# Token-major RWKV values for two groups at once, with the one-token shift through DRAM scratch, in a one-core hybrid attention layer

## The chip, the core and the metric

One core of one Trainium2 chip runs the whole layer as one program. The metric is the device time of one execution in microseconds (us), and of several runs the median. The engines are TensorE (PE in the profile, its weight loads PEld), VectorE (DVE), ScalarE (ACT), GpSimd (POOL) and SyncE (SP), which here only issues DMAs. Each engine works through its own instructions in the order in which the program holds them, and waits on semaphores for the others.

## The reference

A layer of 256 tokens by 2048 features: RMS norm, one wide projection `w_in`, three branches (block attention, an RWKV-7 time mix, attention to a memory), a gated merge and an output projection. The change touches the RWKV branch alone:

```python
def token_shift_lerp(p, mu):
    prev = jnp.pad(p, ((0, 0), (1, 0), (0, 0)))[:, :-1]
    return p + (prev - p) * mu

# rwkv7_time_mix, cut
r = token_shift_lerp(r, mu_r); k = token_shift_lerp(k, mu_k); v = token_shift_lerp(v, mu_v)
...
def step(state, inp):
    r_t, w_t, k_t, v_t, a_t, b_t = inp
    sa = jnp.einsum('bhvk,bhk->bhv', state, a_t)
    state = state * w_t[:, :, None, :] + sa[..., None] * b_t[:, :, None, :] + v_t[..., None] * k_t[:, :, None, :]
    return state, jnp.einsum('bhvk,bhk->bhv', state, r_t)
...
bonus = jnp.sum(rh * kh * r_k, axis=-1, keepdims=True) * vh
```

So v is a projection of the normed input, each token mixed with the token before it by a weight per feature, and is then needed with tokens on the partitions in the recurrence's products and in the bonus.

## The kernel before

**Weights and products.** Every projection is a list of jobs, each cut into chunks of 512 KB of weights. A chunk is loaded by SP (L259, tile `raw`, three buffers), split on ACT into a high part (L270) and on VectorE into the low rest (L273, tile `wt`, four buffers), and multiplied on PE into `pm` tiles of PSUM. In a feature-major job (mode "fm") the weight is stationary and the tokens stream: for each 128 rows one matmul of 512 columns (L308) and one of 256 (L309), over four row blocks and two column halves a chunk. In a wide job the tokens are stationary and 512 weight columns stream three times (L306): 12 matmuls a chunk, and the result has tokens on the partitions.

**Steps and lanes.** After each chunk (`issue_mm`) the loop calls `step_lanes`, which lets every lane, a Python generator, emit its next piece of work; `yield 3` lets three chunks pass. So the order on each engine is the order of emission, and a lane that waits for a flag only emits later.

**The RWKV groups.** Six groups of 256 features (four heads). Per group there are feature-major jobs for R, K and V, whose evacuation (`rkv_evac`, `shift_lerp`) adds the two PSUM parts on POOL (L323), subtracts neighbouring tokens along the free dimension on POOL (L435) and finishes the lerp on VectorE (L431). `pairs_lane` builds decays and keys and ends in a burst of transposes on PE: the squares and r*k sums (L590), then in two tiles V (L599) and both halves of BK (L600, L601), copied to `tok` by ACT (L602) and VectorE (L604). `rw_lane` then makes the gram products (L622, evacuated by VectorE, L626 and L627), sends a 32-column block of them through DRAM (`d1`, `NB`, L652, L663), solves it by forward substitution in many small VectorE instructions (L674, L678, eight steps), and goes on to the products that read V (`from_v` L641, state L751, output L763) and to the group norm (transposes L780, subtraction `Y` L790, L803 on POOL, bonus L805). All small products and transposes share four PSUM tiles named `psd`; a tile is free when its reader is through. `attn_a` holds one from its last product (L876, L878) until its gate is there (L881).

Of the kernel before, what the change touches and what calls it, by code (L numbers as in the profile page):

```python
# [11 lines left out]
FT = mybir.dt.float32  # L12
# [9 lines left out]
NG = 6  # L22
# [16 lines left out]
def tile_hybrid(ctx: ExitStack, tc: tile.TileContext, x, mem, rel_bias, norm_g, mem_norm_g, w_in,  # L39
# [87 lines left out]
    prow2 = load_params((("mur", mu_r, 12), ("muk", mu_k, 12), ("muv", mu_v, 12), ("a0", a0, 12),  # L127
# [248 lines left out]
    def open_p1():  # L376
# [6 lines left out]
        for k in ("XF", "X64", "S"):  # L383
            pool.memset(E[k], 0.0)
        for k in ("lw", "la"):
            E[k] = rw.tile([96, 256], FT, name=k + "_t")

    msk = const.tile([128, 2, 128], FT, name="msk")
    ones = const.tile([128, 1], FT, name="ones")
    fd = dram.tile([HA, 385], FT, name="fd")  # L390
# [61 lines left out]
    def rkv_evac(g, nm, mu):  # L452
# [10 lines left out]
        return f  # L463

# [41 lines left out]
    def pairs_lane(g):  # L506
# [53 lines left out]
        tok = rw.tile([128, 2, 4, 128], FT, name="tok", bufs=2)  # L560
# [22 lines left out]
        yield from wait(("V", g))  # L583
        yield 1
# [9 lines left out]
        v = St.pop(("V", g))  # L594
        for q in range(2):
            p = ps_side()
            pv = p.rearrange("p (a c) -> p a c", a=4)
            for c in range(2):
                pe.transpose(pv[:, c], v[:, q, c * 128:(c + 1) * 128], ident)  # L599
            pe.transpose(pv[:, 2], BK[:, q, 0, 128:256], ident)  # L600
            pe.transpose(pv[:, 3], BK[:, q, 0, 0:128], ident)  # L601
            act.activation(tok[:, q, 0:3], pv[:, 0:3], AF.Copy)  # L602
            for h in range(2):
                dve.tensor_scalar(tok[:, q, 3, 64 * h:64 * h + 64], pv[:, 3, 64 * h:64 * h + 64],  # L604
                                  nb[:, 0, q, h:h + 1], None, op0=OP.mult)
# [4 lines left out]
    def rw_lane(g, AR, BK, tok, nb, bs, esc):  # L610
        rw, GS, XF, X64 = (E[k] for k in ("rw", "GS", "XF", "X64"))
        S = E["S"]
        halves = [slice(64 * h, 64 * h + 64) for h in range(2)]
# [17 lines left out]
        def from_v(c):  # L631
# [4 lines left out]
            for q in range(2):  # L636
# [3 lines left out]
                for h, rows in enumerate(halves):  # L640
                    pe.matmul(pv[:, 2 * q + h], GS[:, c * 4 + 2 * q + h, 2], tok[:, q, c, rows], start=(c == 0), stop=True,  # L641
# [62 lines left out]
        for s in D4[0:2]:  # L704
            act.activation(X64[s, :, s], XN[s], AF.Copy)
        W = from_v(0)
# [29 lines left out]
        for c in range(2):  # L736
# [9 lines left out]
            if c == 0:  # L746
                p = ps_side()
                pv = p[:, 0:128].rearrange("p (q v) -> p q v", q=2)
                for q in range(2):
                    for h, rows in enumerate(halves):  # L750
                        pe.matmul(pv[rows, q], tok[:, q, 2, rows], tok[:, q, 0, rows], start=True, stop=False)  # L751
                        pe.matmul(pv[rows, q], tok[:, q, 3, rows], W[:, 1, q * 2 + h], start=False, stop=True)
# [5 lines left out]
            for q in range(2):  # L758
                if c:
                    pe.matmul(pv[:, q], S[:, q], AR[:, q, 1, 1], start=True, stop=False, skip_group_check=True)  # L760
                for h, rows in enumerate(halves):
                    u = c * 4 + 2 * q + h
                    pe.matmul(pv[rows, q], tok[:, q, c, rows], GS[:, u, 3], start=(c == 0), stop=False,  # L763
# [534 lines left out]
```

## Time and profile before

| | |
|---|---|
| median of three runs | 1477.9 us (1477.35 to 1479.44) |
| profiled execution | 1478.3 us, of which the span from first to last instruction is 1476.5 us |
| PE, PEld, DVE, ACT, POOL busy | 98%, 83%, 64%, 51%, 12% of the span |
| granted TensorE clock | 0.997 of the 2.4 GHz level, over the whole span |
| moved by DMA | 258.9 MB |

Everything the change touches lies in the first half, up to about 740 us; what follows (memory attention, merge, output) is the same text in both kernels. The page's first two parts say who is busy, the chain says what ended last, the table of waits says for whom an engine stood still, and the timeline gives starts, from which the pace of back-to-back instructions is read: a matmul's own duration overlaps its neighbours', the distance of two starts does not.

### The profile page before, as it was taken

What the parts mean: (1) busy time and instruction counts of PE and PEld (TensorE: products, weight loads), DVE (VectorE), ACT (ScalarE), POOL (GpSimd) and SP (SyncE); (2) the same over time, 40 slices, a digit from 0 to 9 for tenths busy, and PEclk for the clock granted to TensorE, in tenths of its full rate; (3) what the DMA queues carried; (4) which work ended last, traced back from release to release, by engine and by line L of the source; (5) the groups of instructions that cost most, each with busy time, mean ns of one, the idle gap of its engine ahead of it and who ended that gap; (6) DMA issues with size and microseconds to landing.
All of it is one profiled execution on the core that took longest, in us unless ns stands there. A gap on an engine that the chain in (4) does not pass through costs nothing.

```text
span 1476.5 us, 22151 instructions
## 1 busy us (share of the span) xinstructions
PE 1449.2 (98%) x8315; PEld 1222.3 (83%) x8315; DVE 946.2 (64%) x1855; ACT 747.3 (51%) x1122; POOL 181.8 (12%) x252
## 2 busy tenths in 40 slices
PE   7999999999999999999999999999999999999997
PEld 6887888888888788788888888888888888888887
DVE  5778697796795786784666555655545545545555
ACT  5546546466456456445666454643443444444443
POOL 4312202212212222211100000000000000000011
PEclk9999999999999999999999999999999999999999
DMA  5665555456465465465575555566556556555753
GB/s 180 192 179 163 159 147 169 143 167 173 133 184 151 134 172 159 135 178 158 162 221 187 172 169 174 167 196 192 187 188 195 188 187 194 188 188 192 262 200 130
DMA packets 207968, 258.88 MB, mean 175 GB/s; under 512 B 28172, under 2 KB 146596, under 8 KB 207220
## 3 DMA queue, kind: packets, MB, share of 16 engines
q1 hardware_dynamic: 201872, 247.11, 54.5%
q10 hardware_dynamic: 4164, 6.71, 1.3%
q0 software_dynamic: 1824, 3.65, 0.8%
q8 instruction: 65, 1.06, 0.3%
q14 instruction: 43, 0.35, 0.1%
HBM read 253.74 MB, written 6.05 MB: 176 GB/s over the span
## 4 chain that ended last, share of the span: by engine, by line
PE 89%; DVE 4%; DMA 2%; ACT 1%; issue 1%; POOL 1%; SPq 0%; ACTq 0%; DVEq 0%
PE pm L306 43%; PE pm L308 24%; PE pm L309 12%; PE psd L622 2%; DVE wt L273 1%; DMA raw<-in_w_in_dram 1%; DVE fs_t L674 1%; PE psd L641 1%; PE psd L1037 1%; PE psd L743 1%; DMA NB<-d 1%; PE psd L154 1%; DMA x_sb<-in_x_dram 1%; ACT wt L270 1%; DVE X L678 1%
## 5 line engine op out<-in xcount | busy, mean ns | idle before, releaser
L273 DVE TENSOR_TENSOR wt<-raw,wt 128x1024 fp32r<-128x1024 f32 (+1 forms) x451 | 559.1, 1242 | 437.4 <-ACT wt L270 433.8
L270 ACT ACTIVATE wt<-raw 128x1024 fp32r<-128x1024 f32 (+1 forms) x452 | 477.2, 1057 | 494.0 <-PE pm L306 256.5
L308 PE MATMUL pm<-hT,wt 128*128 128x512 f32 (+1 forms) x1632 | 587.1, 402 | 0.0
L309 PE MATMUL pm<-hT,wt 128*128 128x256 f32 (+1 forms) x1632 | 458.5, 281 | 3.5 <-DVE wt L273 3.4
L308 PEld LDWEIGHTS pm<-hT,wt 128*128 128x128 f32 (+1 forms) x1632 | 305.7, 187 | 76.3 <-issue 4.2
L306 PE MATMUL pm<-wt,hT 128*128 128x512 f32 x1440 | 335.4, 391 | 0.0
L306 PEld LDWEIGHTS pm<-wt,hT 128*128 128x128 f32 x1440 | 268.6, 188 | 57.6 <-issue 1.7
L309 PEld LDWEIGHTS pm<-hT,wt 128*128 128x128 f32 (+1 forms) x1632 | 307.5, 188 | 6.2 <-DVE wt L273 6.0
L306 PE MATMUL pm<-wt,mg 128*128 128x512 f32 (+1 forms) x384 | 79.3, 367 | 0.0
L306 PEld LDWEIGHTS pm<-wt,mg 128*128 128x128 f32 x384 | 65.7, 189 | 12.5
L1183 POOL MEMSET sso<- 128x16 f32 x1 | 0.1, 117 | 607.0 <-PE pm L306 607.0
L674 DVE TENSOR_TENSOR fs_t<-X,NB 128x30 f32<-128x30 f32 (+13 forms) x354 | 64.9, 223 | 7.5 <-DMA NB<-d 7.1
L306 PE MATMUL pm<-wt,yas 128*128 128x512 f32 x288 | 67.6, 395 | 0.0
L306 PE MATMUL pm<-wt,ybs 128*128 128x512 f32 x288 | 67.6, 395 | 0.0
L323 POOL TENSOR_TENSOR lraw<-lraw,et 128x256 f32<-128x256 f32 (+1 forms) x38 | 45.1, 1207 | 167.2 <-ACT lraw L322 167.2
L306 PEld LDWEIGHTS pm<-wt,ybs 128*128 128x128 f32 x288 | 54.3, 188 | 12.6
L306 PEld LDWEIGHTS pm<-wt,yas 128*128 128x128 f32 x288 | 54.3, 188 | 12.7
L317 ACT ACTIVATE et<-pm 128x256 f32<-128x256 f32 (+1 forms) x112 | 42.6, 382 | 40.3 <-PE pm L309 37.6
L678 DVE TENSOR_TENSOR X<-X,fs_t 128x30 f32<-128x30 f32 (+13 forms) x354 | 56.3, 194 | 0.6
L306 PE MATMUL pm<-wt,mT 128*128 128x512 f32 x192 | 45.8, 395 | 0.0
L308 PE MATMUL pm<-mT,wt 128*128 128x512 f32 x128 | 45.4, 395 | 0.0
L306 PE MATMUL pm<-wt,ycs 128*128 128x512 f32 x192 | 45.3, 395 | 0.0
(299 smaller groups left out, 1324.3 us busy)
## 6 DMA issues: line engine op xcount, KB each, us to landing
raw<-in_w_in_dram SPq DMA_DIRECT2D x320, 512.0 KB, 3.7
raw<-in_w_mem_kv_dram SPq DMA_DIRECT2D x32, 512.0 KB, 3.5
raw<-in_w_out_dram SPq DMA_DIRECT2D x32, 512.0 KB, 4.4
raw<-in_w_proj_a_dram SPq DMA_DIRECT2D x24, 512.0 KB, 4.2
raw<-in_w_proj_b_dram SPq DMA_DIRECT2D x24, 512.0 KB
raw<-in_w_proj_c_dram SPq DMA_DIRECT2D x16, 512.0 KB, 4.4
NB<-d SPq DMA_DIRECT2D x24, 128.0 KB, 3.4
fr<-fd ACTq DMA_DIRECT2D x6, 385.0 KB
```

The source lines that it names most:

```text
L154: pe.transpose(pv[:, a, t], src[:, t, (k + a) * 128:(k + a + 1) * 128], ident)
L270: act.activation(w[:, :, 0], r, AF.Copy)
L273: eng.tensor_tensor(w[:, :, 1], r, w[:, :, 0].bitcast(FT), OP.subtract)
L306: pe.matmul(ps[:, 0:j.n], l, r, start=first and n == 0, stop=last and n == 2)
L308: pe.matmul(ps[0:j.m], hi, both, start=first, stop=last, skip_group_check=True)
L309: pe.matmul(ps[0:j.m, 256:512], lo, top, start=False, stop=last, skip_group_check=True)
L317: act.activation(t, ps[0:j.m, 256:512], AF.Copy)
L323: pool.tensor_tensor(j.dst[f], j.dst[f], t, OP.add)
L622: pe.matmul(pv[h][:, w].rearrange("p x t -> p (x t)"), BK[rows, q, c, w * 128:(w + 1) * 128], AR[rows, q, c].rearrange("p x t -> p (x t)") ...
L641: pe.matmul(pv[:, 2 * q + h], GS[:, c * 4 + 2 * q + h, 2], tok[:, q, c, rows], start=(c == 0), stop=True, skip_group_check=True)
L674: dve.tensor_tensor(t, X[:, k0:8, c:c + 1].to_broadcast([128, m, hi - lo]), NB[:, lo:hi, c].rearrange("p (o n) -> p o n", o=1).to_broadcas ...
L678: dve.tensor_tensor(X[:, k0:8, lo:hi], X[:, k0:8, lo:hi], t, OP.add)
```

## The change

V is computed by three wide jobs (`BJ`), each for two groups, placed after the K job of groups 0, 2 and 4, in place of six feature-major jobs; the attention jobs between are dealt out anew. `v_evac` copies the token-major result to `vt` on ACT. A new lane `v_lane` does the shift: SP stores `vt` to DRAM scratch from row 1 on (row 0 is zero, set once by four POOL DMAs), three steps later SP loads rows 0 to 255 back, so that each token meets the one before it; `mu_v` is loaded onto all partitions by a POOL DMA; three steps later POOL subtracts and multiplies, and two steps after that VectorE adds. V's four transposes per group are gone, and `tok` has two parts and one buffer, for which `pairs_lane` now waits for `half_free` of the group before; it no longer waits for V, `rw_lane` does, just ahead of `from_v`.

```diff
@@ open_p1, scratch
+        for v in vds:
+            for o in (0, 128):
+                pool.dma_start(v[0:1, o:o + 128].rearrange("o (q n) -> o q n", q=2), E["S"][0:1, :, 64:128])
...
+    vds = [dram.tile([257, 256], FT, name="vd%d" % i) for i in range(2)]
@@ new functions
+    def v_evac(g):
+
+        def f(ps, t):
+            if t == 0:
+                if g:
+                    force(("rw", g - 2))
+                for i in range(2):
+                    St["v", g + i] = E["rw"].tile([128, 2, 256], FT, name="vt", bufs=3)
+            for i in range(2):
+                act.activation(St["v", g + i][:, t], two(ps)[:, i], AF.Copy)
+            if t == 1:
+                add_lane(v_lane(g), 2)
+        return f
+
+    def v_lane(g0):
+        for g in (g0, g0 + 1):
+            vt = St["v", g]
+            sh = E["rw"].tile([128, 2, 256], FT, name="vsh")
+            mu = E["rw"].tile([128, 1, 256], FT, name="muv")
+            vd = vds[g % 2]
+            nc.sync.dma_start(vd[1:257].rearrange("(t p) v -> p t v", p=128), vt)
+            pool.dma_start(mu[:, 0], bass.AP(tensor=mu_v.tensor, offset=mu_v.offset + g * 256, ap=[[0, 128], [1, 256]]))
+            yield 3
+            nc.sync.dma_start(sh, vd[0:256].rearrange("(t p) v -> p t v", p=128))
+            yield 3
+            pool.tensor_tensor(sh, sh, vt, OP.subtract)
+            pool.tensor_tensor(sh, sh, mu.to_broadcast([128, 2, 256]), OP.mult)
+            yield 2
+            dve.tensor_tensor(vt, vt, sh, OP.add)
+            flags["V", g] = True
+            yield 1
@@ pairs_lane
-        tok = rw.tile([128, 2, 4, 128], FT, name="tok", bufs=2)
...
-        yield from wait(("V", g))
-        yield 1
+        if g:
+            yield from wait(("half_free", g - 1))
...
-        v = St.pop(("V", g))
+
+        tok = rw.tile([128, 2, 2, 128], FT, name="tok")
+        p = ps_side()
+        pv = p.rearrange("p (a q c) -> p a q c", a=2, q=2)
+        for a in range(2):
+            for q in range(2):
+                pe.transpose(pv[:, a, q], BK[:, q, 0, 128 * (1 - a):128 * (2 - a)], ident)
+        act.activation(tok[:, :, 0], pv[:, 0], AF.Copy)
         for q in range(2):
-            p = ps_side()
-            pv = p.rearrange("p (a c) -> p a c", a=4)
-            for c in range(2):
-                pe.transpose(pv[:, c], v[:, q, c * 128:(c + 1) * 128], ident)
-            pe.transpose(pv[:, 2], BK[:, q, 0, 128:256], ident)
-            pe.transpose(pv[:, 3], BK[:, q, 0, 0:128], ident)
-            act.activation(tok[:, q, 0:3], pv[:, 0:3], AF.Copy)
-            for h in range(2):
-                dve.tensor_scalar(tok[:, q, 3, 64 * h:64 * h + 64], pv[:, 3, 64 * h:64 * h + 64],
-                                  nb[:, 0, q, h:h + 1], None, op0=OP.mult)
+            dve.tensor_tensor(tok[:, q, 1].rearrange("p (h v) -> p h v", h=2), pv[:, 1, q].rearrange("p (h v) -> p h v", h=2),
+                              nb[:, 0, q].rearrange("p (h o) -> p h o", o=1).to_broadcast([128, 2, 64]), OP.mult)
@@ rw_lane, ahead of from_v(0); the products then read vt in place of tok
+        yield from wait(("V", g))
+        vt = St["v", g]
@@ the jobs
-               Job(w_in2, VB + c, 256, 16, hT, rkv_evac(g, "V", "muv"), add=pool),
...
-    for g, (a0_, a1_) in enumerate(((0, 3), (3, 5), (5, 8), (8, 10), (10, 13), (13, 16))):
-        jobs += RJ[4 * g:4 * g + 3] + AJ[a0_:a1_] + RJ[4 * g + 3:4 * g + 4 - (g == NG - 1)]
+    BJ = [Job(w_in2, VB + 512 * i, 512, 16, hT, v_evac(2 * i), mode="wide") for i in range(3)]
+    for g, (a0_, a1_) in enumerate(((0, 2), (2, 5), (5, 7), (7, 10), (10, 12), (12, 16))):
+        jobs += RJ[3 * g:3 * g + 2] + BJ[g // 2:g // 2 + 1 - g % 2] + AJ[a0_:a1_] + RJ[3 * g + 2:3 * g + 3 - (g == NG - 1)]
```

PE's order at group 4's burst of transposes, before (each line or pair of lines with `psd` is one tile; YT is the group norm of group 3):

```order
L309 MATMUL pm<-hT,wt 128x256
L780 MATMUL psd<-ident,YT 128x128 x4
L590 MATMUL psd<-ident,sg 128x128 x4
L590 MATMUL psd<-ident,R 128x128 x4
L599 MATMUL psd<-ident,V 128x128 x2
L600 MATMUL psd<-ident,BK 128x128
L601 MATMUL psd<-ident,BK 128x128
L599 MATMUL psd<-ident,V 128x128 x2
L600 MATMUL psd<-ident,BK 128x128
L601 MATMUL psd<-ident,BK 128x128
L308 MATMUL pm<-hT,wt 128x512
```

And after, where the burst stands between chunks of the wide V job of groups 4 and 5:

```order
L306 MATMUL pm<-wt,hT 128x512 x24
L818 MATMUL psd<-ident,YT 128x128 x4
L626 MATMUL psd<-ident,sg 128x128 x4
L626 MATMUL psd<-ident,R 128x128 x4
L636 MATMUL psd<-ident,BK 128x128 x4
L306 MATMUL pm<-wt,hT 128x512 x12
L658 MATMUL psd<-AR,BK 128x256 x8
```

The burst has four tiles instead of five and 16 transposes instead of 20; the gram products (L622 before, L658 after) follow one chunk later in both. In group 5 the scores of an attention group now stand right behind the burst.

SP's order in group 0, from the gram's block on, before:

```order
L652 DMA d_951<-GS 32x8x32 x4
L259 DMA raw<-in_w_in_dram 128x4x256
L663 DMA NB<-d_951 32x1024 x4
L259 DMA raw<-in_w_in_dram 128x4x256 x9
L682 DMA d_952<-X 256x1x32 x4
```

And after:

```order
L688 DMA d_853<-GS 32x8x32 x4
L259 DMA raw<-in_w_in_dram 128x4x256
L699 DMA NB<-d_853 32x1024 x4
L490 DMA vd_110<-vt 128x2x256
L259 DMA raw<-in_w_in_dram 128x4x256 x3
L493 DMA vsh<-vd_110 128x2x256
L259 DMA raw<-in_w_in_dram 128x4x256 x6
L718 DMA d_854<-X 256x1x32 x4
L490 DMA vd_111<-vt 128x2x256
```

The store of V stands behind the substitution's loads and three weight loads ahead of the shifted load.

VectorE's order in group 0 after the change, where the lerp's addition stands in the forward substitution (L710 and L714 are before's L674 and L678):

```order
L710 TENSOR_TENSOR fs_t<-X,NB 128x14 x2
L714 TENSOR_TENSOR X<-X,fs_t 128x7x2 x2
L498 TENSOR_TENSOR vt<-vt,vsh 128x512
L883 SCALAR_TENSOR_TENSOR as<-psd,bias 128x2x256
L884 SCALAR_TENSOR_TENSOR as<-psd,bias 128x2x128
L889 TENSOR_REDUCE amx<-as 128x2 x2
L273 TENSOR_TENSOR wt<-raw,wt 128x4x256
```

The addition and the softmax's first part stand ahead of a weight split between two column groups of the solve; so it is in group 0, and in groups 2 and 4 the addition lies in the solve too.

## Rows read from the trace of the kernel before

**Rows 1.** The page: busy time and share, and engines of the last chain.

```profile
PE 1449.2 (98%) x8315; PEld 1222.3 (83%) x8315; DVE 946.2 (64%) x1855; ACT 747.3 (51%) x1122; POOL 181.8 (12%) x252
PE 89%; DVE 4%; DMA 2%; ACT 1%; issue 1%; POOL 1%; SPq 0%; ACTq 0%; DVEq 0%
```

**Rows 2.** Whom PE waited for: us in total, times, longest.

```profile
PE pm L309 <- DVE wt L273: 3.4, 5, 0.9
PE psd L599 <- DVE Y L790: 3.4, 5, 0.9
PE psd L622 <- DVE GS L627: 2.3, 4, 0.6
```

**Rows 3.** Windows: stretch, length, busy PE, PEld, DVE, ACT, POOL, clock, DMA, GB/s.

```profile
110.00:131.00 21.00, 18.74 (x102) 15.09 (x101) 19.47 (x91) 13.52 (x24) 4.19 (x7) 1.00 0.52 157
```

**Rows 4.** Timeline of PE in a feature-major job, eight pairs apart.

```profile
427.53 0.39 PE L308 MATMUL pm<-hT,wt 128*128 128x512 f32 x1
...
430.36 0.40 PE L308 MATMUL pm<-hT,wt 128*128 128x512 f32 x1
```

**Rows 5.** Timeline of PE in a wide job: start, us, what, count.

```profile
402.72 16.62 PE L306 MATMUL pm<-wt,hT 128*128 128x512 f32 x72
419.18 0.60 PE L817 MATMUL psd<-ident,Y 128*128 128x128 f32 x4
```

**Rows 6.** Timeline of PE, group 3's burst; in brackets idle time and releaser.

```profile
390.13 0.38 PE L599 MATMUL psd<-ident,V 128*128 128x128 f32 x2
...
390.46 0.27 PE L601 MATMUL psd<-ident,BK 128*128 128x128 f32 x1
391.23 0.41 PE L599 MATMUL psd<-ident,V 128*128 128x128 f32 x2 [0.50 <-DVE Y L790]
```

**Rows 7.** Timeline of PE, group 4's burst and gram products.

```profile
493.83 0.38 PE L590 MATMUL psd<-ident,R 128*128 128x128 f32 x2
495.15 0.41 PE L599 MATMUL psd<-ident,V 128*128 128x128 f32 x2 [0.93 <-DVE Y L790]
...
501.15 1.10 PE L622 MATMUL psd<-AR,BK 64*128 64x256 f32 x6 [0.57 <-DVE GS L627]
```

**Rows 8.** Groups by line and shape: count, busy us, mean ns.

```profile
L431 DVE SCALAR_TENSOR_TENSOR V<-et,par,lraw 128x256 f32<-128x256 f32 x12 | 5.3, 482 | 6.3 <-POOL et L435 6.3
L604 DVE TENSOR_SCALAR tok<-psd,nb 128x64 f32<-128x64 f32 x24 | 5.2, 276 | 0.6
L473 DVE TENSOR_TENSOR zsa<-zsa,et 128x512 f32<-128x512 f32 x6 | 4.1, 683 | 0.0
L803 POOL TENSOR_TENSOR Y<-Y,lnw 128x512 f32<-128x512 f32 x6 | 8.2, 1362 | 87.3 <-issue 53.8 <-DVE Y L801 33.5
```

**Rows 9.** Timelines of VectorE and POOL around 112 us, group 0's solve.

```profile
111.59 0.31 DVE L678 TENSOR_TENSOR X<-X,fs_t 128x33 f32<-128x33 f32 x2
...
112.08 0.85 DVE L678 TENSOR_TENSOR X<-X,fs_t 128x33 f32<-128x33 f32 x2
112.85 0.88 DVE L674 TENSOR_TENSOR fs_t<-X,NB 128x30 f32<-128x30 f32 x2
...
112.14 1.52 POOL L323 TENSOR_TENSOR zsa<-zsa,et 128x256 f32<-128x256 f32 x2 [13.94 <-ACT zsa L322]
```

**Rows 10.** Whom PE waited for between 100 and 140 us.

```profile
PE pm L309 <- DVE wt L273: 2.2, 3, 0.9
```

**Rows 11.** DMA issues: count, size, median us from issue to landing.

```profile
out_dram<-xo SPq DMA_DIRECT2D x4, 256.0 KB, 2.7
...
wd<-in_rw_w_decay_dram POOLq DMA_DIRECT2D x6, 96.0 KB, 3.7
```

**Rows 12.** Timelines of POOL and PE at the start and in V's evacuation.

```profile
35.41 0.53 POOL L515 DMA_DIRECT2D wd<-in_rw_w_decay_dram  x1
42.17 1.03 PE L521 MATMUL psd<-lw_t,wd 96*128 96x256 f32 x4
68.62 6.26 POOL L323 TENSOR_TENSOR lraw<-lraw,et 128x256 f32<-128x256 f32 x2 [4.24 <-ACT lraw L322]
```

More of the change, by code (lines that the diff above doesn't have):

```diff
@@ L126, in tile_hybrid @@
     prow1 = load_params((("g", norm_g, 16),), "1", pool)
-    prow2 = load_params((("mur", mu_r, 12), ("muk", mu_k, 12), ("muv", mu_v, 12), ("a0", a0, 12),
+    prow2 = load_params((("mur", mu_r, 12), ("muk", mu_k, 12), ("a0", a0, 12),
                          ("kk", k_k, 12), ("ka", k_a, 12), ("rk", r_k, 12), ("lnb", lnx_b, 12), ("w0", w0, 12), ("mg", mem_norm_g, 16),
@@ L612, in rw_lane @@
         S = E["S"]
+        vt = None
         halves = [slice(64 * h, 64 * h + 64) for h in range(2)]
@@ L640, in from_v @@
                 for h, rows in enumerate(halves):
-                    pe.matmul(pv[:, 2 * q + h], GS[:, c * 4 + 2 * q + h, 2], tok[:, q, c, rows], start=(c == 0), stop=True,
+                    pe.matmul(pv[:, 2 * q + h], GS[:, c * 4 + 2 * q + h, 2], vt[:, c, 128 * q + 64 * h:128 * q + 64 * h + 64], start=(c == 0), stop=True,
                               skip_group_check=True)
@@ L750, in rw_lane @@
                     for h, rows in enumerate(halves):
-                        pe.matmul(pv[rows, q], tok[:, q, 2, rows], tok[:, q, 0, rows], start=True, stop=False)
-                        pe.matmul(pv[rows, q], tok[:, q, 3, rows], W[:, 1, q * 2 + h], start=False, stop=True)
+                        pe.matmul(pv[rows, q], tok[:, q, 0, rows], vt[:, 0, 128 * q + 64 * h:128 * q + 64 * h + 64], start=True, stop=False)
+                        pe.matmul(pv[rows, q], tok[:, q, 1, rows], W[:, 1, q * 2 + h], start=False, stop=True)
                 for rows in halves:
@@ L762, in rw_lane @@
                     u = c * 4 + 2 * q + h
-                    pe.matmul(pv[rows, q], tok[:, q, c, rows], GS[:, u, 3], start=(c == 0), stop=False,
+                    pe.matmul(pv[rows, q], vt[:, c, 128 * q + 64 * h:128 * q + 64 * h + 64], GS[:, u, 3], start=(c == 0), stop=False,
                               skip_group_check=True)
@@ L806, in rw_lane @@
                 Yq[:, c * 4:c * 4 + 4].rearrange("p (q h) v -> p q h v", q=2),
-                tok[:, :, c].rearrange("p q (h v) -> p q h v", h=2),
+                vt[:, c].rearrange("p (q h v) -> p q h v", q=2, h=2),
                 bs[:, c].rearrange("p q (h o) -> p q h o", o=1).to_broadcast([128, 2, 2, 64]), OP.mult)
```

## The prediction

> **What bounds the kernel now.** Read the page's busy shares and the chain that ended last first: TensorE is busy for 98% of the span, and 89% of the chain is TensorE, most of it the big products L306, L308 and L309 [rows 1]. So time comes off only where PE has fewer columns to stream or waits less. Next, who PE waits for: behind the start it waits 3.4 us for the weight split on VectorE (L273), 3.4 us at the V transposes (L599) for the group norm's subtraction (Y, L790) and 2.3 us at the gram products (L622) for their own evacuation [rows 2]. That is all a faster helper can win. The windows show the other side: in the stretches where VectorE runs the forward substitution (L674, L678), here 110 to 131 us, it is itself busy for 19.47 of 21.00 us [rows 3], and there the weight split is late. An engine with 64% over the span is a second bound in six places.
>
> **The V products (less by 2.0 us).** Six jobs of 32 pairs (512 columns, then 256) become three of 96 matmuls of 512; the columns are the same, the instructions fewer (384 to 288). The feature-major pace: from 427.53 to 430.36 us lie eight pairs, one chunk, 2.83 us [rows 4]. The wide pace: 72 matmuls from 402.72 to 419.18, 16.46 us, so 2.74 us for a chunk of twelve [rows 5]. 24 chunks either way: 24 x 0.083 = 2.0 us, on the path throughout.
> The rows give 229 ns for 512 columns and 354 ns for a 512 and a 256. The Trainium skill, "TensorE: Matmul & The Clock Gate", section "Back-to-back issue gap", has N / 2.4 + 2.5 ns for a matmul of N columns; by it a pair takes 325 ns and the same columns in 512s 324 ns, so an estimate of 0.3 us in all, and a sum of 5.1 instead of 6.8 us. The page does not have the 20 ns that the 256s cost here; the measured pace decides.
>
> **The V transposes (less by 2.6 us).** Three transposes pass from 390.13 to 390.46 us, 0.11 each [rows 6]. V's four per group go, 24 in all: 24 x 0.11 = 2.6 us. The matmuls that read v later (from_v, state, output) keep shape and number: nothing.
>
> **PSUM waits in that burst (less by 3.5 us).** Four side tiles exist. Before, the burst of transposes takes five: YT, two squared sums, two V/BK tiles. So the last one reuses YT's and stands until L790 has read it: 390.46 to 391.23 is 0.77 us where 0.11 would do [rows 6], 0.66 lost. In groups 4 and 5 an attention result holds one of the four (its lane waits for its gate), and already the fourth tile reuses YT's: two transposes from 493.83 should end at 494.05, and L599 starts at 495.15 [rows 7], 1.10 lost. Groups 1 to 3 lose 0.66, groups 4 and 5 lose 1.10: 4.2 us. The new burst takes four tiles. Groups 1 to 3: no reuse, nothing lost. Group 4: the order leaves the attention tile held across the burst, so the fourth still lands on YT's: 1.10 stays. Group 5: no tile is held any more, but the scores products now follow in the same step as a fifth tile; they come 0.44 us (four transposes) later, so 0.65 is lost there. 4.2 - 1.75 = 2.4 us less. The waits at L622 are the same shortage one chunk later, twice in group 4 and twice in group 5, 0.57 each [rows 2, 7]; group 4 keeps its two, group 5 loses its two: 1.1 less. Bounds of this term: nothing (each wait finds another place) and 6.5 (all of 4.2 and 2.3 gone).
>
> **VectorE and POOL (more by 1.3 us).** Per group VectorE loses two lerps (0.482 each) and four 64-column scalings (0.276) and gets two 128-column ones, priced between the 64-column row and L473's 0.68, taken as 0.35, nearer the first since the columns are few, and one 512-column addition at 0.68, as L473 [rows 8]: 2.07 off, 1.38 on. POOL loses two adds and a subtraction and gets two 512-column passes; the nearest row is L803 with 1.36 each [rows 8]. In sum no more than before, but they move: in groups 0, 2 and 4 the passes and the addition fall into the forward substitution. What that costs is in the trace: two POOL adds run from 112.14 to 113.66 and the pairs of small VectorE instructions beside them take 0.85 and 0.88 us instead of 0.31 [rows 9], about 0.55 for each add of 0.76, seven tenths of it. So two passes cost VectorE 0.7 x 2.72 = 1.9 us. Only group 0 is sure to have no cushion (2.2 of the 3.4 us by which PE waits for the split lie there [rows 10]); there 1.9 + 0.68 - 1.37 = 1.3 us reach PE. Lower bound -0.7 (the relief alone reaches PE, once), upper bound three groups at full lock, 3 x (2.72 + 0.68 - 1.37) = 6.1.
> The Trainium skill, "SBUF — State Buffer", section "Who interferes with whom", states that a VectorE instruction with two SBUF inputs and a GpSimd instruction that reads SBUF exclude each other for the whole instruction. By it the upper bound holds in each solve; the row shows seven tenths, so the trace bears the lock out with part of it hidden.
>
> **Round trip, SP and start (nothing).** SP gets a store of 256 KB, three weight loads later the shifted load. A 256 KB store landed in 2.7 us, a POOL load in 3.7 [rows 11]. Three weight loads are three chunks, 8.5 us: the load finds the store landed, and behind it only weight loads queue, which run six or seven chunks ahead of their use. In the order the first product that reads v (from_v) stands seven steps behind group 0's lerp, and further in the others. If the cover were gone: 2.7 us per trip. The store stands behind the substitution's loads in the queue, not ahead. At the start four small POOL DMAs go ahead of the lora sums, about 0.5 us each as the row of L515: w_decay2's load moves from 35.41 to 37.5, lands 3.7 us later [rows 11] at 41.2 and is read at 42.17 [rows 12]: hidden with 1 us left, otherwise at most 1 us.
>
> **Sum.** -2.0 - 2.6 - 3.5 + 1.3 = -6.8. The profiled execution took 1478.3 us, so 1471.5; it lay 0.4 above the median of the runs, so the forecast is 1471.1.
>
> **Rivals.**
> (1) The waits move instead of going: PE's PSUM waits stay at 6.5 us in new places (the scores in group 5 show the way). Then -2.0 - 2.6 + 1.3 = -3.3, 1474.6. For it: VectorE's work in the burst is hardly shorter; against it: four tiles for four uses in groups 1 to 3.
> (2) POOL and VectorE exclude each other in three solves: +6.1 in place of +1.3, that is -2.0, 1475.9. For it: VectorE is full there [rows 3]; against it: PE waits for the split in few places outside group 0.
> (3) Slower: the lerp's last addition (L498) stands in VectorE's strict order two steps, 2 x 2.83 = 5.7 us, behind POOL's first pass. If POOL's pair takes longer, VectorE stops mid-solve with the weight splits queued behind it, and PE starves. POOL did once need 6.26 us for two 256-column V adds beside a busy VectorE [rows 12]; at that rate two 512-column passes take 12.5 us, 6.9 too long, in groups 0, 2 and 4 20.6 us: -8.1 + 20.6 = +12.5, 1490.4. It decides from 9.4 us for the pair on (3.7 too long, three times: 3 us slower). Against it: L803's 1.36 and the idle POOL.
> (4) Only columns count for the V products, since they are the same: no gain from fewer instructions, -4.8, 1473.1. Against it: two paces read over eight pairs and 72 matmuls [rows 4, 5]. The formula in the Trainium skill's TensorE page, above, speaks for it.
> (5) The round trip is not hidden and the lane of a group waits for V, with the rest of its work bunched: about what was saved, 1478.
>
> **How the numbers follow.** No change means within 0.2%, about 3.0 us, so faster ends at 1474.9 and slower begins at 1480.9. Forecast 0.58; rival 1 0.13, half of it on either side of 1474.9; rival 2 0.16; rival 3 0.06; rival 4 0.05; rival 5 0.02. Faster 0.58 + 0.07 + 0.05 = 0.70, same 0.06 + 0.16 + 0.02 = 0.24, slower 0.06. The range: below, all PSUM waits gone and VectorE relieved would be -11.8; 1467.0 leaves that last corner out. Above, rivals 1 and 2 belong in, up to 1478.0.
>
> **What would show it.** V's L306 rows at 229 ns and 96 per job; no L599; the burst without idle time in groups 1 to 3, about 1.1 us at group 4's fourth tile, about 0.65 at group 5's scores; two L622-like waits instead of four; PE's wait for the split between 2.4 and 5 us, in group 0; POOL's two passes under 2 us each. Wrong would be: a wait of VectorE for POOL at L498, of SP for the store, or of PE for the split in groups 2 and 4 by more than 2 us each.

## The result: slower by 0.8%

| | before | after |
|---|---|---|
| median | 1477.7 us (1477.35 to 1479.44, four runs) | 1490.4 us (1487.8 to 1494.2, four runs) |
| ratio | | 1.0082 (95% interval 1.0067 to 1.0097) |
| profiled execution, span | 1478.3, 1476.5 us | 1494.2, 1492.5 us |

The forecast was 1471.1 us, range 1467.0 to 1478.0. The change costs 12.1 us (0.0082 x 1477.7) where 6.8 were to be gained. From the page of the kernel after, to be laid beside [rows 1]: PE's busy line and the shares of the chain that ended last.

```profile
PE 1451.5 (97%) x8195; PEld 1219.5 (82%) x8195; DVE 943.7 (63%) x1837; ACT 737.8 (49%) x1102; POOL 170.7 (11%) x249
PE 76%; DVE 11%; DMA 7%; ACT 2%; issue 2%; SPq 1%; POOL 0%; ACTq 0%; DVEq 0%
```

PE runs 120 matmuls fewer, VectorE is busy 2.5 us less, POOL 11 less: every engine has less to do. (PE's busy time is 2.3 us longer all the same, because stretches of it run at a lower clock, as shown below.) The chain tells the rest: PE's share falls from 89% to 76%, VectorE's rises from 4% to 11% and that of the DMAs from 2% to 7%. Work didn't grow, it became late. Whom PE waits for after the change (us in total, times, longest), against [rows 2]:

```profile
PE pm L309 <- DVE wt L273: 9.4, 11, 1.9
PE psd L736 <- DMA XN<-d: 3.1, 3, 2.5
PE pm L306 <- DVE wt L273: 2.8, 1, 2.8
PE psd L564 <- ACT XF L756: 1.9, 1, 1.9
PE psd L636 <- DVE BK L615: 1.9, 1, 1.9
PE psd L658 <- DVE GS L663: 1.1, 2, 0.6
PE psd L636 <- DVE Y L828: 0.9, 1, 0.9
...
PE psd L876 <- DVE Y L828: 0.5, 1, 0.5
```

The last three lines are the PSUM waits, where the prediction put them: group 4's fourth tile, two gram waits in place of four, group 5's scores. The first five are new or larger. The split (L273) is late for 12.2 us and not 3.4, in groups 0, 2, 3, 4 and 5; the solve's second hop through DRAM (XN), the copy of its result (XF) and the keys of group 0 (BK) are late where nothing was. A single number for the whole: over all pairs of neighbouring matmuls, take by how much the distance of their starts exceeds the median of their form, and add up those of more than 0.5 us. Behind PE's first 20 us that is 12.0 us before and 26.0 us after, called PE's lost time below.

Behind a stall comes a second loss. Four stretches of the windows in which PE is busy throughout (columns as in [rows 3], the clock is the third value from the end):

```profile
124.60:127.80 3.20, 3.20 (x11) 2.71 (x11) 1.26 (x2) 2.58 (x10) 0.00 (x0) 0.50 0.74 209
145.10:148.30 3.20, 3.20 (x12) 2.72 (x11) 3.20 (x6) 1.98 (x4) 2.57 (x3) 0.50 0.22 79
428.40:431.60 3.20, 3.20 (x9) 2.47 (x8) 3.20 (x15) 2.14 (x4) 0.00 (x0) 0.50 0.64 172
568.40:571.60 3.20, 3.20 (x12) 2.72 (x12) 1.87 (x2) 3.05 (x7) 2.89 (x5) 0.50 0.77 223
```

The granted clock is 0.50, 1.2 GHz, each time some us after PE stood for 2 to 3 us (the stall of 1.9 us for BK at 72 us left it at the full clock); pairs of products then start 0.64 us apart and not 0.35. The trace of before has no such stretch between its start and its end. The parts nearly add up: 14.0 us more of lost time, an estimate of 1.4 us for each of the four stretches shown (3.20 us at 0.35 / 0.64 of the pace), less the 4.6 us forecast for the V products and transposes, make 15.0 of the 16.0 us between the two spans. It is one trace: how many such stretches there are differs from run to run, and the median lies 3.7 us below this execution.

### The profile page after: what moved, and what is told of

Same layout as the page of the kernel before. It is cut to its first block, busy times and chain, and to the rows that moved or that the text cites. A ratio compares the mean times of both kernels' runs of the same rounds, so it can differ in the third digit from the quotient of the medians.

```text
span 1492.5 us, 21895 instructions
## 1 busy us (share of the span) xinstructions
PE 1451.5 (97%) x8195; PEld 1219.5 (82%) x8195; DVE 943.7 (63%) x1837; ACT 737.8 (49%) x1102; POOL 170.7 (11%) x249
## 4 chain that ended last, share of the span: by engine, by line
PE 76%; DVE 11%; DMA 7%; ACT 2%; issue 2%; SPq 1%; POOL 0%; ACTq 0%; DVEq 0%
PE pm L306 43%; PE pm L308 15%; PE pm L309 8%; DVE wt L273 4%; DVE fs_t L710 3%; DMA raw<-in_w_in_dram 3%; DVE X L714 2%; DMA NB<-d 1%; PE psd L658 1%; ACT wt L270 1%; DMA d<-GS 1%; PE psd L1075 1%; PE psd L781 1%; DMA XN<-d 1%; PE psd L154 1%
## 5 line engine op out<-in xcount | busy, mean ns | idle before, releaser
L273 DVE TENSOR_TENSOR wt<-raw,wt 128x1024 fp32r<-128x1024 f32 (+1 forms) x451 | 555.7, 1235 | 456.0 <-ACT wt L270 453.4
L308 PE MATMUL pm<-hT,wt 128*128 128x512 f32 (+1 forms) x1440 | 522.0, 404 | 0.0
L309 PE MATMUL pm<-hT,wt 128*128 128x256 f32 (+1 forms) x1440 | 407.9, 283 | 9.5 <-DVE wt L273 9.4
L306 PE MATMUL pm<-wt,hT 128*128 128x512 f32 x1728 | 407.3, 393 | 2.8 <-DVE wt L273 2.8
L306 PEld LDWEIGHTS pm<-wt,hT 128*128 128x128 f32 x1728 | 322.5, 189 | 73.8 <-issue 3.7
L308 PEld LDWEIGHTS pm<-hT,wt 128*128 128x128 f32 (+1 forms) x1440 | 272.4, 189 | 66.2 <-issue 2.4
L309 PEld LDWEIGHTS pm<-hT,wt 128*128 128x128 f32 (+1 forms) x1440 | 274.2, 190 | 14.1 <-DVE wt L273 13.8
L306 PE MATMUL pm<-wt,mg 128*128 128x512 f32 (+1 forms) x384 | 79.3, 367 | 0.0
L306 PEld LDWEIGHTS pm<-wt,mg 128*128 128x128 f32 x384 | 65.7, 189 | 12.5
L710 DVE TENSOR_TENSOR fs_t<-X,NB 128x30 f32<-128x30 f32 (+13 forms) x354 | 65.5, 224 | 11.6 <-DMA NB<-d 11.1
L306 PE MATMUL pm<-wt,yas 128*128 128x512 f32 x288 | 67.6, 395 | 0.0
L306 PE MATMUL pm<-wt,ybs 128*128 128x512 f32 x288 | 67.6, 395 | 0.0
L306 PEld LDWEIGHTS pm<-wt,ybs 128*128 128x128 f32 x288 | 54.3, 189 | 12.6
L306 PEld LDWEIGHTS pm<-wt,yas 128*128 128x128 f32 x288 | 54.3, 189 | 12.6
L714 DVE TENSOR_TENSOR X<-X,fs_t 128x30 f32<-128x30 f32 (+13 forms) x354 | 60.3, 206 | 0.6
L317 ACT ACTIVATE et<-pm 128x256 f32<-128x256 f32 (+1 forms) x100 | 38.0, 382 | 43.9 <-PE pm L309 39.2
L306 PE MATMUL pm<-wt,mT 128*128 128x512 f32 x192 | 45.8, 396 | 0.0
L306 PE MATMUL pm<-wt,ycs 128*128 128x512 f32 x192 | 45.3, 395 | 0.0
L306 PEld LDWEIGHTS pm<-wt,ycs 128*128 128x128 f32 x192 | 36.2, 189 | 8.4
```

The source lines that it names most:

```text
L273: eng.tensor_tensor(w[:, :, 1], r, w[:, :, 0].bitcast(FT), OP.subtract)
L306: pe.matmul(ps[:, 0:j.n], l, r, start=first and n == 0, stop=last and n == 2)
L308: pe.matmul(ps[0:j.m], hi, both, start=first, stop=last, skip_group_check=True)
L309: pe.matmul(ps[0:j.m, 256:512], lo, top, start=False, stop=last, skip_group_check=True)
L317: act.activation(t, ps[0:j.m, 256:512], AF.Copy)
L710: dve.tensor_tensor(t, X[:, k0:8, c:c + 1].to_broadcast([128, m, hi - lo]), NB[:, lo:hi, c].rearrange("p (o n) -> p o n", o=1).to_broadcas ...
```

## What the lane costs: four runs

The first theory was that the lane's transfers block SP and the solve's DRAM hops. The rivals: its sums on POOL and VectorE, or the new order of the attention jobs. One run drops the lane, one its transfers, one its sums, one moves the transfers.

```diff
 no_lane: v_lane only sets the flags
 no_trip:
-            nc.sync.dma_start(vd[1:257]...)  /  nc.sync.dma_start(sh, vd[0:256]...)
-            pool.tensor_tensor(sh, sh, vt, OP.subtract)
+            pool.tensor_tensor(sh, vt, vt, OP.subtract)
 no_lerp: the two pool.tensor_tensor and the dve.tensor_tensor of the lane are left out
 trips_early: both stores first, load 1 two steps later, sums two steps later, then load 2
```

> Leaves out the shift of the values: no store, no load, no mu row, no subtraction, product or addition of the lane; V goes to its users unshifted. Before is 1477.7 us, after 1490.4. Theory T (the lane's transfers stand between the two DRAM hops that end the solve, in groups 0, 2 and 4, and hold up these hops and the raw weights; after a stall PE runs at its lower clock): about 1477 us, since the stalls at 137 to 148, 563 and their low clock go, and those of group 0 at 120.7 and of group 3 at 424 stay. Rival O (the order of the attention work alone, scores and spread rows in the solves): 1486 or more, the lane is nearly free. Rival L (the lane's POOL and VectorE work in the solves): 1477 too, told apart by the next two runs.

> Leaves out the round trip: neither store nor load; the lane's subtraction, product, addition and mu row stay, on V itself (so the shift is left out). Theory T: about 1479 us, within 2 us of the run without the lane. Rival L: within 2 us of after, 1488 to 1491. Rival O: 1486 or more.

> Keeps both transfers and the mu row of the lane and leaves out its POOL subtraction and product and its VectorE addition (the shift is left out). Theory T: 1487 to 1490 us, since only 6 additions of 0.69 us go, half of them where VectorE is full. Rival L: about 1478. Rival O: 1486 or more, as in the other two runs.

> Computes all of it. Both stores at the lane's start, the first load two steps later, the second behind the first addition, so that no transfer of the lane stands between d<-X and XN<-d; VectorE's and POOL's work is the same and lies in the solve. Theory T: faster than after by the stalls behind the solves of groups 0, 2 and 4, 4 to 8 us, so 1482 to 1486; XN<-d lands in under 3 us again. Rivals L and O: 1490, or more, since more of the lane now falls in the solve.

| run | ratio to before | 95% interval |
|---|---|---|
| no_lane | 1.0041 | 1.0026 to 1.0056 |
| no_trip | 1.0076 | 1.0057 to 1.0094 |
| no_lerp | 1.0044 | 1.0031 to 1.0057 |
| trips_early | 1.0115 | 1.0102 to 1.0129 |

Each interval is 0.0013 to 0.0019 wide on either side, so the difference of two runs is known to about 0.002, 3 us. The theory fell. Without transfers the time hardly moves (0.0006); without the sums it moves as far as without the lane, 0.0038, 5.6 us. In trips_early both pairs of POOL passes lie in the solve, and it is slower by 0.0033. What the sums do is seen in the timelines of VectorE and POOL in the kernel after, group 0's solve, just where [rows 9] were read:

```profile
103.30 0.31 DVE L714 TENSOR_TENSOR X<-X,fs_t 128x33 f32<-128x33 f32 x2
103.53 1.43 DVE L710 TENSOR_TENSOR fs_t<-X,NB 128x30 f32<-128x30 f32 x2
104.88 1.39 DVE L714 TENSOR_TENSOR X<-X,fs_t 128x30 f32<-128x30 f32 x2
...
103.46 1.30 POOL L495 TENSOR_TENSOR vsh<-vsh,vt 128x512 f32<-128x512 f32 x1 [3.60 <-DMA vsh<-vd]
104.84 1.29 POOL L496 TENSOR_TENSOR vsh<-vsh,muv 128x512 f32<-128x512 f32 x1
```

Two column instructions take 0.31 us; with a POOL pass of 1.30 beside them they take 1.43, and with the next 1.39. VectorE's instruction ends when POOL's does: 1.1 us lost for each pass, 2.2 for a lane, in groups 0, 2 and 4 alike (103.46, 316.96 and 536.22 us). This is called the lock below. The Trainium skill, "SBUF — State Buffer", section "Who interferes with whom", states that a VectorE instruction with two SBUF inputs and a GpSimd instruction that reads SBUF exclude each other. The trace agrees with it in full.

The seven tenths that the prediction took in its place came from a merged row. Taken apart, the first pair of [rows 9] is one instruction that began before POOL's add and took its usual 0.19 us, and one that began behind it and lasted until the add ended:

```profile
112.14 0.74 POOL L323 TENSOR_TENSOR zsa<-zsa,et 128x256 f32<-128x256 f32 x1 [13.94 <-ACT zsa L322]
112.19 0.73 DVE L678 TENSOR_TENSOR X<-X,fs_t 128x30 f32<-128x30 f32 x1
```

So what is lost is POOL's pass less the 0.19 us that VectorE's instruction takes anyway: 0.55 of 0.74 us there, 1.1 of 1.30 here. It is no fixed share of the pass.

The other half of the loss, 0.0041, is there without the lane.

## Three single edits and a new deal

```diff
 spread_early (attn_a)
-            later(4, spread_rows, g + 1)
+            later(1 if g == 2 else 4, spread_rows, g + 1)
 scores0_late
+    AJ[1:3] = AJ[2], AJ[1]
 lerp_behind (v_lane)
-            yield 3        # between load and sums
+            yield 8 if g == g0 else 3
-            yield 2        # between sums and addition
+            yield 1
 dealt: spreads at 1; the lane of groups 0 and 1 as in lerp_behind; per group between K and Z of RWKV
+ 0: V01, Q0, Z0   1: KA0, Q1, V23   2: KA1, VA01, Z1   3: Q2, KA2, V45   4: Q3, KA3, VA23   5: Q4, KA4, Z2, Z3   (end cut)
```

> Computes all of it. One DMA stands elsewhere: the spread of the bias rows for attention pair 3 (fr<-fd) is issued three steps earlier, so that it doesn't start 0.6 us ahead of group 3's first DRAM hop (d<-GS, 406.73 us, 7.0 us to landing). Theory S (the spread holds up the hop, NB<-d stands behind it on SP's queue, the raw weights behind NB<-d, and PE waits 3.0 us at 424.03 and runs at 1.2 GHz from 428.3 to 431.7): after less 3 to 5 us, 1485.5 to 1487.5; d<-GS of group 3 lands in under 4 us. Rival: the hop is late for another cause, or the stall returns elsewhere: within 1.5 us of after, 1490.

> Computes all of it. Of the attention jobs KA and ZA of pair 0 change places, so that the first softmax (2.1 us of VectorE at 120 us) stands behind the solve of group 0 and not in it. Theory F (VectorE is full in a solve: whatever else is put there makes the split late, and PE waits): after less the stall at 120.73 us (2.2 us) and its low clock (about 1.7 us), so 1486 to 1487. Rival: the stall stays, since the raw weights or the addition of the lane make it: 1489 to 1491.

> Computes all of it. In the lane of a pair the first group's subtraction, product and addition stand behind the last column of the solve and not in its middle, and the second group's transfers and sums behind these. Theory L (the lane's sums inside the solve cost, by VectorE's time and by what POOL takes from it): the same as the run without the sums, 1.0044 of before, so 1484 to 1486. Rival: it is the sums themselves wherever they stand, or they now hold up XF's copies on POOL and with them PE: 1489 or more.

> Computes all of it. The V job of groups 2 and 3 stands in group 1's part, that of groups 4 and 5 in group 3's, so that their lanes are done before the next solve begins; the lane of groups 0 and 1 has its sums behind the solve; the attention jobs are dealt so that no softmax starts inside a solve, and the spreads stand three steps earlier. If the solves' fullness is the cause of both halves of the loss (theories F, L and S together): 0.994 to 0.998 of before, 1469 to 1475 us where before is 1477.7. If wide V products or the shorter burst cost by themselves: 1.002 or more.

| run | ratio | 95% interval |
|---|---|---|
| spread_early | 1.0055 | 1.0041 to 1.0070 |
| scores0_late | 1.0085 | 1.0071 to 1.0098 |
| lerp_behind | 1.0021 | 1.0009 to 1.0034 |
| dealt | 0.9951 | 0.9939 to 0.9963 |

Spread_early gives 0.0027, 4.0 us, as theory S said. In group 3, which has no V job and no lane in its solve, ACT's queue sends out the bias rows (`fr<-fd`, 385 KB in many short rows) just ahead of the solve's first hop on SP's queue. From the timelines of ACT and SP in the kernel after:

```profile
406.15 0.60 ACTq L426 DMA_DIRECT2D fr<-fd  x1
406.73 1.96 SPq L688 DMA_DIRECT2D d<-GS  x4
```

The median landing of that hop, in the stretch 405 to 427 us (DMA issues: count, size, us to landing):

```profile
d<-GS SPq DMA_DIRECT2D x4, 32.0 KB, 7.0
```

SP's waits in group 3 of the same kernel, for the load behind the hop:

```profile
SPq L699 <- DMA d<-GS: 6.4, 1, 6.4
```

And its timelines of VectorE, which waits for that load, of ACT and of PE:

```profile
424.26 0.28 DVE L710 TENSOR_TENSOR fs_t<-X,NB 128x16 f32<-128x16 f32 x2 [5.78 <-DMA NB<-d]
...
425.95 1.22 DVE L273 TENSOR_TENSOR wt<-raw,wt 128x1024 fp32r<-128x1024 f32 x1
...
419.90 1.06 ACT L270 ACTIVATE wt<-raw 128x1024 fp32r<-128x1024 f32 x1 [2.72 <-DMA raw<-in_w_in_dram]
...
427.22 4.20 PE L306 MATMUL pm<-wt,hT 128*128 128x512 f32 x11 [2.80 <-DVE wt L273]
```

It is one chain: SP stands on the hop for 6.4 us and issues the load of NB late; VectorE stands for 5.78 us until NB lands; and the next weight split, whose raw weights and ACT half were there at 420.96 us, stands in VectorE's order behind the first columns of the solve until 425.95. PE stands for 2.8 us. (Raw weights queue behind the hop too, but here they aren't what comes last.) In spread_early the spread leaves at 388.73 us and the hop at 401.71; it lands in 3.9 us (median of the same four), and SP's wait is gone:

```profile
SPq L699 <- DMA d<-GS: 0.2, 1, 0.2
```

Scores0_late moves the first softmax out of the solve and gains nothing: theory F, that anything put on VectorE there costs its duration, fell for the time as a whole. Its trace shows why one should be careful with a single stall: the one of 2.2 us at 121 us is gone, and in its place stand 1.0 us at 110 us and 1.1 and 0.8 us for XN at 130. Lerp_behind gains 0.0061, more than dropping the sums (0.0038). It also moves the second group's transfers, and the two intervals overlap at their ends, so nothing is built on the difference. Dealt, which computes all of it, is faster than both kernels, by 7.2 us where 6.8 were forecast for the change; but its order of jobs is another one than after's, so it doesn't bear out the forecast.

## Which engine, which part

```diff
 lerp_on_dve: the lane's two passes
-            pool.tensor_tensor(...)
+            dve.tensor_tensor(...)
 behind_spread = lerp_behind + spread_early
 lane_away = the V jobs and lanes of dealt, spreads at 4, the attention's scores at the chunks of after
 away_spread = lane_away with spreads at 1
 before_scores_in (kernel before)
+    AJ[0:3] = AJ[2], AJ[0], AJ[1]
+    AJ[5:7] = AJ[6], AJ[5]
```

> Computes all of it. The lane's subtraction and product are made on VectorE in the same places of the program, and not on POOL. Theory P (while POOL runs one of them, 1.30 us, VectorE stands: a column operation of 0.18 us that starts under it takes 1.30 us, 1.1 us lost for each, 2.2 us for each lane): VectorE loses 2 x 0.69 = 1.4 us in place of 2.2, in three solves 2.5 us less, so 1.005 to 1.0075 of before (after: 1.0082). Rival: POOL's work ran beside VectorE's and cost nothing, the addition alone did: 4 to 8 us more than after, 1.010 to 1.013.

> Computes all of it. Both single edits at once: the lane's sums behind the solve (1.0021 of before) and the spread for attention pair 3 three steps earlier (1.0055, where after was 1.0082). If their causes are separate, 1.0021 - 0.0027 = 0.9994, bounds 0.998 to 1.001; if both removed one and the same stall, 1.002.

> Computes all of it. The V jobs and the lanes stand as in the run with the new deal (0.9951), while the attention's scores come at the same chunks as in after (28, 80, 104, 156, 168, 176) and the spreads stand as in after. If the lanes in the solves are the larger part: 0.998 to 1.002 (0.9951, 0.0027 for the spread, up to 0.004 for softmax in solves 0, 2 and 5). If the attention work in the solves is the larger part: 1.004 or more.

> The kernel before with two changes of order: Z, Q, KA of attention pair 0 and Z, KA of pair 1 change places, so that the scores of pairs 0 and 1 come at chunks 28 and 80, as in after (before: 24 and 76), inside the solves of groups 0 and 2. If softmax work in a solve costs (theory F): 3 to 6 us, 1.002 to 1.004. If it doesn't: 0.999 to 1.001, and what is lost in after beside the lane and the spread is of the new kernel alone.

> Computes all of it. The run with the V jobs away from the solves and the attention dealt as in after (0.9995), and now the spreads three steps earlier, as in the run with the new deal (0.9951). It differs from that run by the order of the attention jobs alone. If the spread was the whole difference: 0.994 to 0.996. If the attention work in the solves of groups 0, 2 and 5 has a price in this kernel: 0.9995 - 0.0027 = 0.997, bounds 0.996 to 0.998.

| run | ratio | 95% interval |
|---|---|---|
| lerp_on_dve | 1.0055 | 1.0042 to 1.0068 |
| behind_spread | 0.9987 | 0.9974 to 1.0000 |
| lane_away | 0.9995 | 0.9986 to 1.0004 |
| before_scores_in | 0.9997 | 0.9987 to 1.0007 |
| away_spread | 0.9987 | 0.9979 to 0.9996 |

Lerp_on_dve gives VectorE 1.4 us more work in each lane and is 0.0027 faster than after: the wait for POOL was dearer than the work. Lane_away, with the scores and spreads as in after, stands at 0.9995: the place of the V jobs and lanes is worth 0.0087 there, more than the whole lane costs (0.0041). The attention jobs between stand in another order too, so this isn't the price of the sums alone. The two single edits of behind_spread add up (0.9994 expected, 0.9987 found). Before_scores_in says that in the kernel before the softmax of pairs 0 and 1 is free inside a solve. Away_spread gained 0.0008 where 0.0027 was expected and ends 0.0036 behind dealt, from which it differs by the attention's order alone. Its waits of PE have one that lane_away's have not:

```profile
PE psd L876 <- POOL ka L323: 4.9, 2, 3.0
```

Group 3's stall is gone, but the scores in the solves of groups 0 and 5 (109 and 636 us) now wait for POOL, which adds up KA. The timelines of ACT and POOL for the first of the two:

```profile
109.80 1.06 ACT L270 ACTIVATE wt<-raw 128x1024 fp32r<-128x1024 f32 x1 [5.58 <-PE pm L309]
...
111.49 1.20 POOL L323 TENSOR_TENSOR ka<-ka,et 128x256 f32<-128x256 f32 x1 [13.73 <-ACT ka L322]
```

PE has nothing to do from 109.70 us on. ACT splits a chunk of weights, which had waited 5.58 us for PE to free a buffer, and only then copies KA; so POOL starts at 111.49. Its add takes 1.20 us where the same add took 0.74 in after (107.66 us), because VectorE's split runs until 112.11: the lock from its other side, 0.46 us of a wait of 3.0. At 636 us it is 0.73 us of 1.8. In dealt no scores stand in a solve, and this wait is absent. So scores in the solves of groups 0 and 2 cost the kernel before nothing, while in this order of the new kernel they cost something. If that holds for after too, the two kernels differ in what a solve can bear.

## The place of the solves

One line of the change had not been tried. `pairs_lane` no longer waits for V and rests a step, so burst, hops and solve of every group are issued two chunks earlier: the solve's columns at chunks 22 to 29 of each period of 28, and not at 24 to 31, counted in the program's order. The jobs, spreads and scores around them did not move along. Solve_late puts two steps of rest there and leaves all else of after as it is; late_no_lane does so in no_lane.

```diff
 solve_late (pairs_lane; solve_later4 has 4)
+        yield 2
         if g:
             yield from wait(("half_free", g - 1))
 late_no_lane, late_behind, late_dealt: the same line in no_lane, lerp_behind, dealt
 (with yield 10 for yield 8 in the last two)
```

> Computes all of it. After, with two steps of rest where the pair lane waited for V before, so that burst, hops and solve of every group stand two chunks later, as in the kernel before; the lane of V stays in the solves of groups 0, 2 and 4. If the solves' earlier place is what makes group 3's hop meet the spread: after less 3 to 5 us, 1.0045 to 1.006, and no wait of SP for d<-GS above 2 us. If the earlier place had no part in it: 1.007 to 1.010.

> Leaves out the shift of the values, as the first run without the lane (1.0041), with the solves two chunks later. Theory R (with the solves where before has them, VectorE enters each with its splits 5 to 6 us ahead of PE, as before, and only the lane's sums in three solves are new): what was forecast for PE's own work, 1477.7 - 8.1 = 1469.6 us, 0.9935 to 0.9955 of before. If the wide V jobs have a price of their own: 0.997 or more.

> Computes all of it. The solves two chunks later and the lane's first sums behind the last column. Theory R: PE loses under 2 us in each solve, 0.994 to 0.996 of before. If the sums cost nothing where VectorE is well ahead: the same as solve_late, 0.9965 to 0.9975.

> Computes all of it. The new deal (0.9951) with the solves two chunks later. If the deal and the place of the solves remove the same losses: 0.994 to 0.996. If each removes its own: 0.991 to 0.993.

> Computes all of it. After with four steps of rest in place of two (solve_late: 0.9970). If the later place is good in itself, because VectorE catches up longer after the burst: 0.995 to 0.997. If two chunks is the place that the job ends, the spread and the scores leave free: 0.998 to 1.002.

| run | ratio | 95% interval |
|---|---|---|
| solve_late | 0.9970 | 0.9958 to 0.9981 |
| late_no_lane | 0.9940 | 0.9927 to 0.9952 |
| late_behind | 1.0002 | 0.9993 to 1.0011 |
| late_dealt | 0.9962 | 0.9949 to 0.9976 |
| solve_later4 | 1.0064 | 1.0051 to 1.0076 |

One line turns 0.8% slower into 0.3% faster. Four runs make a square:

| | with the lane | without it | the lane |
|---|---|---|---|
| solves two chunks early | 1.0082 | 1.0041 | 0.0041, 6.1 us |
| solves where before has them | 0.9970 | 0.9940 | 0.0030, 4.4 us |
| the place | 0.0112, 16.6 us | 0.0101, 14.9 us | |

Within the intervals the place costs the same with the lane and without, and the lane the same in either place. PE's waits in solve_late, to be laid beside those of after above (line numbers are higher by one from there on):

```profile
PE pm L309 <- DVE wt L273: 6.8, 7, 2.0
...
PE psd L915 <- ACT pT L908: 1.4, 1, 1.4
PE psd L659 <- DVE GS L664: 1.1, 2, 0.6
PE psd L637 <- DVE Y L829: 0.9, 1, 0.9
```

The waits for BK, XF, XN and the one at L306 are gone, the split's is down to 6.8 us (before: 3.4), no stretch between start and end is at 1.2 GHz, and PE's lost time behind the first 20 us is 12.3 us, as before. Here the longest wait of SP for d<-GS in group 3 is 2.0 us; elsewhere there is one of 2.7, more than was expected. The spread of the bias rows, which the edit doesn't touch, is again 12.1 us ahead of group 3's hop:

```profile
394.19 0.60 ACTq L426 DMA_DIRECT2D fr<-fd  x1
...
406.25 1.96 SPq L689 DMA_DIRECT2D d<-GS  x4
```

In before the two leave at 394.76 and 406.86 us.

What makes the place bad? One part is shown by its own run, the spread that meets group 3's hop (4.0 us). For the rest there is a reading of the trace only, and it is not shown. VectorE's splits run ahead of PE, and this lead has to pay for the solve. Two chunks into the solves of groups 2, 3 and 4 the lead (end of the chunk's L273 to PE's first use of it) is 4.6, 4.2 and 3.5 us before, 2.5, 1.6 and 2.5 after, 5.4, 4.2 and 4.1 in solve_late. The reading is that with 1 to 3 us less in hand the lock and the softmax reach PE and the hops come late. Two things speak against taking it for the whole cause. In groups 0 and 1 the lead hardly tells after from solve_late (6.2 and 5.8, 6.0 and 6.0 us), and yet group 0's XF makes PE wait for 1.9 us in after alone. And in dealt the lead is 1.6 us in groups 3 and 4 as well, and in neither solve does PE wait for the split (group 5, at 1.8, has one such wait of 1.3): a small lead costs nothing in these two solves, into which no spread, lane or softmax falls. So a small lead goes with the loss, but not by itself; which of the neighbours counts for how much wasn't isolated. Later isn't better in itself either: solve_later4 stands at 1.0064, with a wait of PE behind the solve, for the first product's copy Z, that after has at 1.0 us:

```profile
PE pm L309 <- DVE wt L273: 8.6, 7, 3.7
PE psd L752 <- ACT Z L740: 7.0, 3, 3.0
```

Late_behind missed by most: the sums behind the last column, with the solves late, should have given 0.995 and gave 1.0002. Its timelines of VectorE and POOL at the end of group 0's solve:

```profile
126.34 2.06 DVE L715 TENSOR_TENSOR X<-X,fs_t 128x16 f32<-128x16 f32 x1
128.43 0.17 DVE L711 TENSOR_TENSOR fs_t<-X,NB 128x8 f32<-128x8 f32 x1
128.63 1.12 DVE L715 TENSOR_TENSOR X<-X,fs_t 128x8 f32<-128x8 f32 x1
...
127.06 1.29 POOL L495 TENSOR_TENSOR vsh<-vsh,vt 128x512 f32<-128x512 f32 x1
128.43 1.29 POOL L496 TENSOR_TENSOR vsh<-vsh,muv 128x512 f32<-128x512 f32 x1
```

The passes are written behind the last column, but only VectorE is behind with its list; POOL has nothing ahead that holds it, reaches the passes early and locks the last columns, the ones that the hop waits for. (The first of them, 2.06 us, began 0.7 us ahead of the pass and was held all the same; what held it until then isn't shown.) The split stands behind these columns, and PE waits 3.1 us for it. The late deal (0.9962) and the early one (0.9951) overlap, as expected if deal and place cure the same loss by two ways. Dealt is the fastest full version by its median, 1470.5 us at the before of the first measurement (0.9951 x 1477.7). PE's waits there:

```profile
PE psd L658 <- DVE GS L663: 2.0, 2, 1.0
PE pm L309 <- DVE wt L273: 1.8, 2, 1.3
PE psd L636 <- DVE BK L615: 1.6, 1, 1.6
PE psd L626 <- DVE Y L828: 1.4, 1, 1.4
```

## Why the prediction was wrong, step by step

**V products, transposes, PSUM waits (-2.0, -2.6, -3.5).** Right as a sum. Late_no_lane has these three terms without the lane and without the earlier solves: 8.9 us less (7.1 to 10.8), forecast 8.1. It also has V's lerps off POOL and VectorE and the new deal of the attention jobs, so the single terms are read from the trace of after. V's products start 227 ns apart (median) there, as the wide jobs of before do; the idle time of PE for PSUM is 2.5 us (0.9, 1.1 and 0.5) against 5.7 (3.4 and 2.3), in the groups and at the sizes named. Rivals 1 and 4 (the waits move, only columns count) fall with these two readings, and their sums, 4.6 us for the first and 6.1 for the second, lie below the interval. (A chunk gains 2.83 - 16.46 / 6 = 0.087 us by the rows, not 0.083: 2.1 us.)

**VectorE and POOL (+1.3, bounds -0.7 to 6.1).** Mis-sized. The lane costs 4.4 us with the solves in their old place and 6.1 in the new one. (The sum itself slips: 1.9 + 0.68 - 1.37 is 1.2.) Two choices failed. One is seven tenths of the pass for the lock, where VectorE loses the pass less 0.19 us, 2.2 a lane and not 1.9. The other weighs more: "only group 0 is sure to have no cushion", when with the solves early PE also waits for the split in groups 2, 3, 4 and 5. This is the mechanism of rival 2; its price of 6.1 agrees with the lane's, within some 3 us either way, but comes on top of a larger loss.

**Round trip, SP and start (nothing).** Right as far as it goes. Without the transfers (no_trip) the time is the same within the intervals. The start came as priced: w_decay2's load is issued at 37.13 us, and PE reads it at 42.95 without a wait. What the term doesn't have is that group 0's burst now stands 1.9 us for BK; in solve_late, two chunks later, that wait is gone.

**The step that failed.** The text ahead of the prediction says that `rw_lane` and no longer `pairs_lane` waits for V, and the prediction prices what a lane loses by waiting (rival 5). It does not ask what a lane does that waits less: it moves, with all its DMAs and VectorE work, two chunks past jobs, spreads and scores that stay. The sum puts this at nothing, without a reason. The square shows 16.6 us for it (14.9 without the lane), more than all priced terms together. Of these, 4.0 us are the spread ahead of group 3's hop; how the rest divides stays open.

**Rival 3** named 1490.4 us, and the median is 1490.4, but by coincidence. It has VectorE standing at L498 for POOL; after has no such wait, and the pair took 1.30 and 1.29 us, 2.6 together, far from the 9.4 from which the rival decides. Of the signs that were to show the forecast wrong, one came: PE waits for the split by more than 2 us in group 2 (three stalls of 1.0 to 1.3 us at 321 to 337) and in group 4 (0.5 to 1.4, four of them at 539 to 554).

## What to carry to other kernels

A wait that is taken out moves everything behind it: list what the freed work now stands beside, its DMAs and those of the other queues too, before the saved work is counted. Where a helper's lead pays for a busy stretch, measure the lead at the entry and what falls into the stretch: with 1.6 us of lead two solves went through without a wait for the split when nothing else stood in them, and others lost time when a spread or a lane did. And a place in the program holds an engine back only if that engine's own list is late: to keep two engines apart, give one of them a real dependence or put the work on one of the two.

## What the runs showed of the hardware

- A POOL pass of 512 columns (1.30 us) with two SBUF inputs holds a VectorE instruction of 0.18 us until it ends (after, 103.46 us); moving both passes of every lane to VectorE itself made the kernel 0.0027 faster (lerp_on_dve). The other way round, a VectorE split stretched a POOL add from 0.74 to 1.20 and 1.47 us (away_spread, 111.49 and 636.66 us).
- A transfer of 385 KB in short rows on ACT's queue issued 0.6 us ahead made four 32 KB hops of SP's queue land in 7.0 us (median, after) and not 3.9 (spread_early, where it left 13 us ahead).
- After stalls of PE of 2 to 3 us the clock fell to 1.2 GHz in four places of after. It isn't a fixed price: solve_late kept the full clock after a stall of 2.3 us (119 us), no_lane had 6.7 us of the low one (554.3 to 561.0) after one of 2.0, and dealt fell to it once (595 us) after stalls of 1.5 and 1.2.
